# A two-block transformer on one core: 16-blocks of the recurrence's inverses solved four head pairs at a time beside the projections, and 512 moving columns in block 1

## The chip, the cores and the metric

The kernel runs on one core of a Trainium2 chip. The metric is the device time of one execution in microseconds (us). Each kernel is run several times and the median counts. Engines are named as in the profile: PE is TensorE, DVE VectorE, ACT ScalarE, POOL GpSimd, and SP the engine whose queue issues the weight loads.

## What is computed

Two blocks follow one another on a sequence of 256 tokens of width 1024. Block 1 has two layers with three branches each (differential attention, a gated spatial unit, windowed attention), whose inputs are one large projection. Block 2 has two layers between four feed-forward stages; its second layer is an RWKV-7 time mix. This is the part of the reference that the larger edit touches:

```python
xr, xw, xk, xv, xa, xg = [h + xx * mu[i] for i in range(6)]
r = xr @ w_r;  k = xk @ w_k;  v = xv @ w_v
a = jax.nn.sigmoid(a0 + (xa @ a1) @ a2)
g = jax.nn.sigmoid(xg @ g1) @ g2
kk = l2_normalize((k * k_k).reshape(B_, L, H, N))
k = k * (1 + (a - 1) * k_a)
...
def step(S, inp):
    r_t, w_t, k_t, v_t, a_t, b_t = inp
    sa = jnp.einsum('bhvk,bhk->bhv', S, a_t)
    S = S * w_t[:, :, None, :] + sa[..., None] * b_t[:, :, None, :] + v_t[..., None] * k_t[:, :, None, :]
    return S, jnp.einsum('bhvk,bhk->bhv', S, r_t)
```

The recurrence has 16 heads of 64 and 272 steps (16 extra tokens stand ahead of the 256). The kernel computes it in five chunks of 64 steps; within a chunk the dependence of each step on the earlier ones is a triangular system, and its inverse is formed explicitly.

## The kernel before

Activations stay in SBUF, features on partitions: `h` is 128 x 8 x 272. Each weight matmul is three fp32r matmuls, of a high and a low half of either side (`mm3`, L218 to L220; in pinned stretches the same instructions carry L96, and in block 1 `proj_tok` issues them itself). Weights stream in units of 128x1024 f32: SP loads `wraw`, ACT copies the high half `wh` (L210), and DVE, or POOL where the stream says so, subtracts to get the low half `wl` (L212). A unit feeds 24 matmuls. There are four `wraw` buffers and three each of `wh` and `wl`.

A scheduler orders the instructions of each engine, except those pinned to program order. The stages in the profiled execution, in us from the span's start, are: block 1 (9 to 636), a feed-forward (640 to 832), the hybrid layer (832 to 1055), two feed-forwards (1055 to 1467), the RWKV layer's front (1467 to 1602), its eight head pairs (1602 to 1812), its output projection (1812 to 1838), and the last feed-forward with the final norm.

**Block 1.** `proj_tok` forms token-major projections, seven per layer in two layers: each has two PSUM tiles of 128 x 512, and writes half of one (256 columns, two pieces of 128) per matmul.

**The RWKV front.** Projections k, r and v take eight units each, those of the two-step gates (`lora`) a few more. Their inputs are mixes of neighbouring tokens (`mixt` L1523 on DVE; the low half `xl` or `xml` L1526 on DVE and POOL by turns). Behind the decay gate stand a scan (L1565, DVE) and two POOL operations on `D_all` (L1567, L1568). Then kk is normalised and multiplied out (`kt` L1599, `kp` L1600, `kk` L1601 on DVE, `ba_all` L1602 on POOL).

**The head pairs.** A loop runs `stage_b(s-1)`, `stage_c(s-3)`, `stage_a(s)` for eight pairs, so that pairs overlap. `stage_a` makes the decayed operands (L1664 to L1669), the matrix products of a chunk (L1677) with their masked copies (L1681 keeps the 16-blocks in `fk`, L1684, L1687), and sums the 16-blocks into `Uc` (L1690). `stage_b` is `tri_inverse`: the copy L920 and 15 steps of three DVE operations each (L923 to L925) invert the 16-blocks of one pair, 128 partitions x 5 chunks x 16; L927 spreads them into `iY`, and PE and DVE double them to 32 and 64 (L937 to L951). `stage_c` runs the state through the chunks (L1720 to L1737) and normalises (L1743 on); its last instruction is L1763 on POOL.

The steps of the elimination, whose width grows by five elements each:

```python
for j in range(15, 0, -1):
    sh = T(c, pool, [n, ni, 16], F32, f"ish{par}", bufs=2)[:, :, j:]
    nc.vector.stream_shuffle(sh, Yc[:, :, j:], [(p // 16) * 16 + j for p in range(32)])
    nc.vector.tensor_mul(sh, sh, Uc[:, :, j:j + 1].to_broadcast([n, ni, 16 - j]))
    nc.vector.tensor_add(Yc[:, :, j:], Yc[:, :, j:], sh)
```

Of the kernel before, what the change touches and what calls it, by code (L numbers as in the profile page):

```python
# [371 lines left out]
def block1_layer(c, l, xT, head, pos, ws, w_br, w_out, sgu_w, sgu_b, sgu_gb):  # L372
# [14 lines left out]
    def proj_tok(evac):

        pss = [bank(c), bank(c)]
        for p in range(2):  # L390
            for kh in range(2):
                wh, wl = next_unit()
                wh4 = wh.rearrange("p (m k c) -> p m k c", m=2, k=4)
                wl4 = wl.rearrange("p (m k c) -> p m k c", m=2, k=4)
                for i in range(2):
                    o = pss[i][:, 256 * p:256 * p + 256].rearrange("p (m c) -> p m c", m=2)
                    for k4 in range(4):
                        k = 4 * kh + k4
                        a, b = xh[:, k, P * i:P * i + P], xl[:, k, P * i:P * i + P]
                        h, w = wh4[:, :, k4, :], wl4[:, :, k4, :]  # L400
                        pe.matmul(o, a, h, start=k == 0, stop=False)
                        pe.matmul(o, a, w, start=False, stop=False)
                        pe.matmul(o, b, h, start=False, stop=k == 7)
                        if p and kh and k4 == 3:
                            evac(i, pss[i])
                        yield
# [503 lines left out]
def tri_inverse(c, pool, U, Uc, n, ni, levels, nl=None, ybufs=1, tag="sm", par="", pe=None, waits=(0, 0)):  # L910
# [8 lines left out]
    Yc = T(c, pool, [n, ni, 16], F32, f"iYc{par}")  # L919
    nc.vector.tensor_copy(Yc, c.e16[:n].unsqueeze(1).to_broadcast([n, ni, 16]))  # L920
    for j in range(15, 0, -1):
        sh = T(c, pool, [n, ni, 16], F32, f"ish{par}", bufs=2)[:, :, j:]
        nc.vector.stream_shuffle(sh, Yc[:, :, j:], [(p // 16) * 16 + j for p in range(32)])  # L923
        nc.vector.tensor_mul(sh, sh, Uc[:, :, j:j + 1].to_broadcast([n, ni, 16 - j]))  # L924
        nc.vector.tensor_add(Yc[:, :, j:], Yc[:, :, j:], sh)  # L925
# [553 lines left out]
def rwkv(c, h, acc, a):  # L1479
# [20 lines left out]
    with ExitStack() as fst:  # L1500
# [40 lines left out]
        def proj8(q, x, nm):
            for j in range(KT):
                ps = proj(*wrkv.unit(KT * q + j), x)
                nc.scalar.activation(tok(nm, j), ps, AF.Copy)

# [41 lines left out]

        keep = tc.keep_in_program_order
        keep(nc.scalar.preload_act_table_set("natural_log_exp_and_others"))
        for j in range(KT):  # L1590
            ps = bank(c, "sm")
            nc.tensor.matmul(ps[:, :TOK2], c.bo, tok("g", j), start=True, stop=True)
            keep(nc.scalar.activation(tok("g", j), ps[:, :TOK2], AF.Ln, bias=c.eps1))
            keep(nc.scalar.activation(tok("g", j), tok("g", j), AF.Exp, scale=-0.5))
        proj8(2, mix(3), "v")

        for j in range(KT):
            t = T(c, fp, [P, TOK2], F32, "kt1", bufs=2)
            nc.vector.tensor_scalar(t, tok("ba", j), col(c, "k_a", j), c.hc[:, 2, j:j + 1], ALU.mult, ALU.add)  # L1599
            nc.vector.tensor_mul(tok("kp", j), tok("kk", j), t)  # L1600
            nc.vector.scalar_tensor_tensor(tok("kk", j), tok("kk", j), col(c, "k_k", j), tok("g", j), ALU.mult, ALU.mult)  # L1601
            nc.gpsimd.tensor_mul(tok("ba", j), tok("ba", j), tok("kk", j))  # L1602
# [361 lines left out]
```

## Time and profile before

| | |
|---|---|
| median of 3 runs | 2035.62 us (2034.56 to 2041.07) |
| the profiled execution | 2033.22 us, span 2031.5 us, mean granted PE clock 0.964 |
| PE busy | 1929.5 us, 95% of the span, 15003 matmuls |
| DVE busy | 1390.8 us, 68% |
| ACT busy | 973.2 us, 48% |
| POOL busy | 285.1 us, 14% |
| RWKV front and pairs | 1467 to 1812 us of the span |

Busy PE time is modelled for pipelined matmuls, so prices of matmuls are read from the distance between the starts of neighbours. A busy time on DVE or POOL includes what an instruction waited for within itself. The clock is a share of the full 2.4 GHz: 0.5 is 1.2 GHz.

### The profile page before, as it was taken

The page shows a single profiled execution, that of the slowest core. Times are in us where ns is not written, and L with a number is a line of the kernel's source. Part 1 is how long each engine was busy: PE and PEld are TensorE (multiplying, and loading weights), DVE is VectorE, ACT ScalarE, POOL GpSimd, SP SyncE. Part 2 cuts the span into 40 slices and gives each one's busy share as a digit, 9 for nine tenths or more (in the row PEclk, how much of TensorE's full clock was granted, in tenths as well). Part 3 has the DMA queues.
Part 4 walks back from the last instruction along what each step waited for, and adds up shares of the span by engine and source line. Part 5 has one row for each costly group of instructions (what it writes and reads, how often), then busy time and mean ns, then how long its engine had stood idle before and what let it go on. Part 6 is the DMA issues. An engine that isn't in the chain of part 4 may idle for free.

```text
span 2031.5 us, 37801 instructions
## 1 busy us (share of the span) xinstructions
PE 1929.5 (95%) x15003; PEld 1858.0 (91%) x15003; DVE 1390.8 (68%) x2896; ACT 973.2 (48%) x1745; POOL 285.1 (14%) x320
## 2 busy tenths in 40 slices
PE   8999999999999999968999999999989879989998
PEld 7889999889999999966999999999988768979998
DVE  6577576577578665787477665666589699846764
ACT  5455355455355444442354444444366535555443
POOL 1113011113010000143010000000044313110000
PEclk9999899999899999987999999999989789989999
DMA  6445466445455555532235555555534100026663
GB/s 200 137 123 160 142 180 181 142 117 161 141 177 176 177 175 174 164 107 63 63 112 169 175 175 176 171 175 174 171 94 135 42 12 1 32 72 180 186 186 115
DMA packets 79461, 280.02 MB, mean 138 GB/s; under 512 B 9890, under 2 KB 12082, under 8 KB 79156
## 3 DMA queue, kind: packets, MB, share of 16 engines
q1 hardware_dynamic: 77088, 275.57, 45.5%
q8 instruction: 118, 1.93, 0.4%
q10 hardware_dynamic: 2196, 2.03, 0.3%
q14 instruction: 59, 0.48, 0.1%
HBM read 276.50 MB, written 1.07 MB: 137 GB/s over the span
## 4 chain that ended last, share of the span: by engine, by line
PE 64%; DVE 9%; ACT 2%; POOL 2%; issue 1%; DVEq 0%; ACTq 0%; POOLq 0%
PE mm L220 17%; PE mm L218 16%; PE mm L219 16%; PE mm L96 4%; PE iv L96 1%; PE iv L946 1%; DVE wl L212 1%; PE fs L96 1%; PE sm L1677 1%; DVE mixt L1523 1%; DVE iYc L925 1%; DVE ish L924 1%; DVE ish L923 0%; PE sm L264 0%; ACT wh L210 0%
## 5 line engine op out<-in xcount | busy, mean ns | idle before, releaser
L210 ACT ACTIVATE wh<-wraw 128x1024 fp32r<-128x1024 f32 x517 | 546.9, 1059 | 603.6 <-PE mm L219 288.8
L212 DVE TENSOR_TENSOR wl<-wraw,wh 128x1024 fp32r<-128x1024 f32 x474 | 587.1, 1239 | 254.9 <-ACT wh L210 249.6
L218 PE MATMUL mm<-xh,wh 128*128 128x272 f32 (+1 forms) x2112 | 607.4, 288 | 5.9 <-ACT xh L1524 3.0
L220 PE MATMUL mm<-xh,wl 128*128 128x272 f32 (+1 forms) x2112 | 606.2, 287 | 6.6 <-DVE wl L212 2.9
L219 PE MATMUL mm<-xl,wh 128*128 128x272 f32 (+1 forms) x2112 | 606.9, 287 | 0.9 <-POOL xl L1526 0.9
L220 PEld LDWEIGHTS mm<-xh,wl 128*128 128x128 f32 x2112 | 401.5, 190 | 9.0 <-DVE wl L212 5.1
L218 PEld LDWEIGHTS mm<-xh,wh 128*128 128x128 f32 x2112 | 399.7, 189 | 7.9 <-ACT xh L1524 3.5
L219 PEld LDWEIGHTS mm<-xl,wh 128*128 128x128 f32 x2112 | 401.1, 190 | 1.9 <-POOL xl L1526 1.3
L218 PE MATMUL mm<-uh,wh 128*128 128x272 f32 (+1 forms) x704 | 201.7, 286 | 0.0
L219 PE MATMUL mm<-ul,wh 128*128 128x272 f32 (+1 forms) x704 | 201.5, 286 | 0.0
L220 PE MATMUL mm<-uh,wl 128*128 128x272 f32 (+1 forms) x704 | 201.0, 286 | 0.0
L212 POOL TENSOR_TENSOR wl<-wraw,wh 128x1024 fp32r<-128x1024 f32 x43 | 103.0, 2396 | 412.4 <-ACT wh L210 368.8
L96 PE MATMUL mm<-wh,xh 128*128 128x256 f32 x448 | 133.9, 299 | 9.2 <-ACT wh L210 9.2
L220 PEld LDWEIGHTS mm<-uh,wl 128*128 128x128 f32 x704 | 133.2, 189 | 0.0
L218 PEld LDWEIGHTS mm<-uh,wh 128*128 128x128 f32 x704 | 132.3, 188 | 0.0
L219 PEld LDWEIGHTS mm<-ul,wh 128*128 128x128 f32 x704 | 132.3, 188 | 0.0
L96 PE MATMUL mm<-wl,xh 128*128 128x256 f32 x448 | 127.4, 284 | 0.7 <-DVE wl L212 0.7
L96 PE MATMUL mm<-wh,xl 128*128 128x256 f32 x448 | 126.6, 283 | 0.0
L96 PE MATMUL mm<-xh,wh 128*128 128x272 f32 (+1 forms) x360 | 120.0, 333 | 0.0
L96 PE MATMUL mm<-xh,wl 128*128 128x272 f32 (+1 forms) x360 | 107.0, 297 | 0.0
L96 PE MATMUL mm<-xl,wh 128*128 128x272 f32 (+1 forms) x360 | 106.8, 297 | 0.0
L96 PEld LDWEIGHTS mm<-wh,xh 128*128 128x128 f32 x448 | 86.1, 192 | 9.2 <-ACT wh L210 9.2
(597 smaller groups left out, 3576.9 us busy)
## 6 DMA issues: line engine op xcount, KB each, us to landing
wraw<-in_ffn_in SPq DMA_DIRECT2D x176, 512.0 KB, 3.6
wraw<-in_w_in SPq DMA_DIRECT2D x136, 512.0 KB, 3.7
wraw<-in_ffn_out SPq DMA_DIRECT2D x88, 512.0 KB, 3.7
wraw<-in_hyb_in SPq DMA_DIRECT2D x29, 512.0 KB, 3.7
wraw<-in_w_br SPq DMA_DIRECT2D x24, 512.0 KB, 3.8
wraw<-in_rw_rkv SPq DMA_DIRECT2D x24, 512.0 KB, 3.8
wraw<-in_w_out SPq DMA_DIRECT2D x16, 512.0 KB, 4.4
wraw<-in_hyb_out SPq DMA_DIRECT2D x8, 512.0 KB, 3.7
```

What stands on the lines that cost most here:

```text
L96: return lambda *a, **k: self.tc.keep_in_program_order(f(*a, **k))
L210: nc.scalar.activation(wh, r, AF.Copy)
L212: eng.tensor_sub(wl, r, wh.bitcast(F32))
L218: pe.matmul(ps, lh, rh, start=start, stop=False)
L219: pe.matmul(ps, lh, rl, start=False, stop=False)
L220: pe.matmul(ps, ll, rh, start=False, stop=stop)
L924: nc.vector.tensor_mul(sh, sh, Uc[:, :, j:j + 1].to_broadcast([n, ni, 16 - j]))
L925: nc.vector.tensor_add(Yc[:, :, j:], Yc[:, :, j:], sh)
L946: pe.matmul(ps[:n, n * i:n * i + n], lhs[:, i0 + i, :], rhs[:, i0 + i, :], start=True, stop=True)
L1523: nc.vector.scalar_tensor_tensor(t, xx[:, k, :], col(c, "mu", 8 * i + k), hn[:, k, 1:], ALU.mult, ALU.add)
L1677: nc.tensor.matmul(ps[:, P * q:P * q + P], pair_ht(bd[:, c0 + q]), pair_ht(AR[:, c0 + q]), start=True, stop=True)
```

## The change

**Block 1.** `proj_tok` writes 512 contiguous moving columns per matmul, a whole PSUM tile, instead of 256 in two pieces: 48 matmuls per call instead of 96, over the same four units. The host lays the units out accordingly (two k-blocks by four column blocks each).

**The RWKV layer.** The elimination leaves `tri_inverse` and becomes the generator `eliminate`. For the head pairs it runs in the front, for four pairs at once on a tile of 128 x 20 x 16: the first group five steps at a time in the last three turns of the loop over r's units, the second two steps per unit of v. What it needs is made there too: `normed(j)` and `blocks(j)` run per pair in the loop over r, where `blocks` has two exponentials (ACT), three products (DVE), five matmuls of 64 columns, the masked copy out of PSUM and the sum into `Uc` (DVE). `stage_a` loses the masked copy and the sum, but not the decayed operands, which are made a second time. The addend `kt` moves from DVE to ACT. The `wl` subtractions of r's and v's sixteen units move from DVE to POOL. In program order r moves behind the gates' projections. The hybrid layer calls the same `eliminate` in one piece, as before.

```diff
-        for p in range(2):
-            for kh in range(2):
-                wh, wl = next_unit()
...
-                    o = pss[i][:, 256 * p:256 * p + 256].rearrange("p (m c) -> p m c", m=2)
...
+        for kq in range(4):
+            wh, wl = next_unit()
+            for i in range(2):
+                for k2 in range(2):
+                    k = 2 * kq + k2
+                    a, b = xh[:, k, P * i:P * i + P], xl[:, k, P * i:P * i + P]
+                    h, w = wh[:, 512 * k2:512 * k2 + 512], wl[:, 512 * k2:512 * k2 + 512]
+                    pe.matmul(pss[i], a, h, start=k == 0, stop=False)
+                    pe.matmul(pss[i], a, w, start=False, stop=False)
+                    yield
+                    pe.matmul(pss[i], b, h, start=False, stop=k == 7)
...
+def eliminate(c, pool, Uc, Yc, n, ni):
+
+    nc = c.nc
+    nc.vector.tensor_copy(Yc, c.e16[:n].unsqueeze(1).to_broadcast([n, ni, 16]))
+    for j in range(15, 0, -1):
+        sh = T(c, pool, [n, ni, 16], F32, "ish", bufs=2)[:, :, j:]
+        nc.vector.stream_shuffle(sh, Yc[:, :, j:], [(p // 16) * 16 + j for p in range(32)])
+        nc.vector.tensor_mul(sh, sh, Uc[:, :, j:j + 1].to_broadcast([n, ni, 16 - j]))
+        nc.vector.tensor_add(Yc[:, :, j:], Yc[:, :, j:], sh)
+        yield
...
-        lora1, lora2, wrkv = Stream(c, a["rw_lora1"]), Stream(c, a["rw_lora2"]), Stream(c, a["rw_rkv"])
+        lora1, lora2 = Stream(c, a["rw_lora1"]), Stream(c, a["rw_lora2"])
+        wrkv = Stream(c, a["rw_rkv"], lambda u: u >= KT)
...
+        def normed(j):
...
+            nc.scalar.activation(t, tok("ba", j), AF.Identity, scale=col(c, "k_a", j), bias=c.hc[:, 2, j:j + 1])
+            nc.vector.tensor_mul(tok("kp", j), tok("kk", j), t)
...
+        def blocks(j, Uc):
+
+            D = Dall[:, j]
+            E1 = T(c, fp, [P, NCH, 64], F32, "lds", bufs=2)
+            nc.scalar.activation(E1, D[:, :, :64], AF.Exp)
+            E2 = T(c, fp, [P, NCH, 64], F32, "ldc", bufs=2)
+            nc.scalar.activation(E2, D[:, :, 1:], AF.Exp, scale=-1.0)
+            nc.vector.scalar_tensor_tensor(E1, chv("kk", j), -1.0, E1, ALU.mult, ALU.mult)
+            for q in range(2):
+                s = slice(64 * q, 64 * q + 64)
+                nc.vector.tensor_mul(bbd[s, :, q, :], chv("ba", j)[s], E2[s])
+            ps = bank(c, "sm")
+            for q in range(NCH):
+                nc.tensor.matmul(ps[:, 64 * q:64 * q + 64], bbd[:, q].rearrange("p h t -> p (h t)"), E1[:, q],
+                                 start=True, stop=True)
+            U16 = T(c, fp, [P, NCH, 64], F32, "U16")
+            nc.vector.tensor_mul(U16, ps[:, :RT].rearrange("p (c t) -> p c t", t=64),
+                                 c.m16.unsqueeze(1).to_broadcast([P, NCH, 64]))
+            nc.vector.tensor_reduce(Uc, U16.rearrange("p i (b c) -> p i c b", c=16), AX.X, ALU.add)
+
+        Ucs = [T(c, fp, [P, 4 * NCH, 16], F32, f"Uc{i}") for i in range(2)]
+        steps = []
+        for j in range(KT):
+            normed(j)
+            if j >= 1:
+                blocks(j - 1, Ucs[(j - 1) // 4][:, NCH * ((j - 1) % 4):NCH * ((j - 1) % 4) + NCH])
+            if j == 5:
+                steps = eliminate(c, fp, Ucs[0], Ycs[0], P, 4 * NCH)
+            for _ in range(5):
+                next(iter(steps), None)
+            ps = proj(*wrkv.unit(KT + j), xr)
+            nc.scalar.activation(tok("r", j), ps, AF.Copy)
+        blocks(7, Ucs[1][:, 3 * NCH:])
+        steps = eliminate(c, fp, Ucs[1], Ycs[1], P, 4 * NCH)
+        for j in range(KT):
+            for _ in range(2):
+                next(steps, None)
+            ps = proj(*wrkv.unit(2 * KT + j), xv)
+            nc.scalar.activation(tok("v", j), ps, AF.Copy)
```

**Where the order shows it.** The first place is DVE in the front while PE works on v. Before, in this stretch (`kt`, `kp`, `kk` as above, `mixt` and `xml` for the input of the last gate):

```order
L1599 TENSOR_SCALAR kt_3232_18561<-ba_all_17238,cols_80,hcols_16531 128x272
L1601 SCALAR_TENSOR_TENSOR kk_3002_17252<-kk_3002_17252,cols_80,g_all_17241 128x272
L1600 TENSOR_TENSOR kp_3011_17261<-kk_3003_17253,kt_3232_18561 128x272
L1523 SCALAR_TENSOR_TENSOR mixt_18568<-xx_17305,cols_80,hn_17304 128x272
L212 TENSOR_TENSOR wl_18433<-wraw_18430,wh_18432 128x1024
L1601 SCALAR_TENSOR_TENSOR kk_3003_17253<-kk_3003_17253,cols_80,g_all_17241 128x272
L1526 TENSOR_TENSOR xml_18567<-mixt_18568,xmh_18566 128x272
L1523 SCALAR_TENSOR_TENSOR mixt_18572<-xx_17305,cols_80,hn_17304 128x272
```

In the changed kernel, where the lines of `eliminate` are L913 to L915 and the two groups' tiles are the two `Yc`:

```order
L913 STREAM_SHUFFLE ish_17887<-Yc_3013_16608 128x20x15
L913 STREAM_SHUFFLE ish_17940<-Yc_3014_16609 128x20
L914 TENSOR_TENSOR ish_17887<-ish_17887,Uc_3176_17420 128x20x15
L914 TENSOR_TENSOR ish_17940<-ish_17940,Uc_3177_17421 128x20
L915 TENSOR_TENSOR Yc_3013_16608<-Yc_3013_16608,ish_17887 128x20x15
L915 TENSOR_TENSOR Yc_3014_16609<-Yc_3014_16609,ish_17940 128x20
L913 STREAM_SHUFFLE ish_17944<-Yc_3014_16609 128x20x2
L914 TENSOR_TENSOR ish_17944<-ish_17944,Uc_3177_17421 128x20x2
```

The stretch now holds the end of the first group's elimination and, from the second step on, the second group's alone; the low halves `wl` of v are gone from it, and those of the last two gate units come at the second group's steps 11 and 13.

The second place is POOL at the same time. Before (`ba_all` is the last product of the normalisation, the MEMSET clears tiles for the pairs):

```order
L1602 TENSOR_TENSOR ba_all_17238<-ba_all_17238,kk_3002_17252 128x272
L1602 TENSOR_TENSOR ba_all_17238<-ba_all_17238,kk_3003_17253 128x272
L1526 TENSOR_TENSOR xml_18567<-mixt_18572,xmh_18566 128x272
L1526 TENSOR_TENSOR xml_18567<-mixt_18580,xmh_18566 128x272
L1526 TENSOR_TENSOR xml_18567<-mixt_18588,xmh_18566 128x272
L1526 TENSOR_TENSOR xml_18567<-mixt_18596,xmh_18566 128x272
L1644 MEMSET wraw_18757 128x640
```

In the changed kernel, from r's third unit on (`ba_all` is L1614 there):

```order
L212 TENSOR_TENSOR wl_17548<-wraw_17545,wh_17547 128x1024
L1614 TENSOR_TENSOR ba_all_16566<-ba_all_16566,kk_2998_16576 128x272
L212 TENSOR_TENSOR wl_17605<-wraw_17602,wh_17604 128x1024
L212 TENSOR_TENSOR wl_17662<-wraw_17659,wh_17661 128x1024
L212 TENSOR_TENSOR wl_17740<-wraw_17737,wh_17739 128x1024
L1614 TENSOR_TENSOR ba_all_16566<-ba_all_16566,kk_2999_16577 128x272
L212 TENSOR_TENSOR wl_17817<-wraw_17814,wh_17816 128x1024
L1614 TENSOR_TENSOR ba_all_16566<-ba_all_16566,kk_3000_16578 128x272
```

POOL's row now carries the sixteen 128x1024 subtractions of r and v among the eight `ba_all` products, each of which the blocks of a pair wait for.

## Rows read from the trace of the kernel before

**Rows 1.** Windows: stretch, its length, busy us (instructions) of PE, PEld, DVE, ACT, POOL, PE clock, DMA share, GB/s

```profile
1526.90:1591.40 64.50, 60.29 (x437) 58.69 (x438) 58.60 (x89) 42.36 (x82) 31.14 (x29) 0.95 0.42 131
1602.00:1676.00 74.00, 56.21 (x320) 48.96 (x321) 63.79 (x309) 26.07 (x67) 14.78 (x20) 0.73 0.02 8
1676.00:1755.00 79.00, 74.46 (x594) 68.89 (x593) 73.30 (x328) 44.21 (x126) 21.93 (x28) 1.00 0.03 8
1755.00:1812.00 57.00, 47.74 (x363) 43.39 (x362) 22.85 (x69) 28.31 (x79) 12.07 (x16) 0.97 0.12 38
```

**Rows 2.** Timeline of PE in block 1: start us, us, engine, line, operation

```profile
11.09 0.41 PE L96 MATMUL mm<-wh,xh 128*128 128x256 f32 x1
...
16.43 0.41 PE L96 MATMUL mm<-wl,xh 128*128 128x256 f32 x1
...
30.73 0.28 PE L96 MATMUL mm<-wl,xh 128*128 128x256 f32 x1
...
37.44 0.28 PE L96 MATMUL mm<-wl,xh 128*128 128x256 f32 x1
```

**Rows 3.** Windows: one stretch of a feed-forward, columns as in the first group

```profile
700.00:800.00 100.00, 100.00 (x800) 100.00 (x799) 63.45 (x90) 48.11 (x65) 0.00 (x0) 1.00 0.59 175
```

**Rows 4.** Timeline of POOL, 112 to 116 us

```profile
112.88 2.37 POOL L212 TENSOR_TENSOR wl<-wraw,wh 128x1024 fp32r<-128x1024 f32 x1 [16.85 <-ACT wh L210]
```

**Rows 5.** Timeline of DVE, the same stretch

```profile
113.09 2.44 DVE L484 SCALAR_TENSOR_TENSOR gate<-gt,ga 128x256 f32<-128x256 f32 x1
```

**Rows 6.** Source line L484: count, min/median/max ns, first and last start

```profile
L484 DVE SCALAR_TENSOR_TENSOR gate<-gt,ga x12: 410/418/2483, 113.1 to 267.2; 128x256 f32<-128x256 f32 x12
```

**Rows 7.** Timeline of DVE in the hybrid layer, its elimination

```profile
932.61 0.20 DVE L923 STREAM_SHUFFLE ish<-iYc 96x36 f32<-96x36 f32 x1
...
933.31 0.20 DVE L923 STREAM_SHUFFLE ish<-iYc 96x48 f32<-96x48 f32 x1
...
946.57 1.66 DVE L924 TENSOR_TENSOR ish<-ish,iUc 96x120 f32<-96x120 f32 x1
...
948.59 0.31 DVE L923 STREAM_SHUFFLE ish<-iYc 96x132 f32<-96x132 f32 x1
...
949.26 0.29 DVE L925 TENSOR_TENSOR iYc<-iYc,ish 96x132 f32<-96x132 f32 x1
```

**Rows 8.** Timeline of DVE in the front (neighbours of one kind merged, xcount)

```profile
1542.34 2.35 DVE L212 TENSOR_TENSOR wl<-wraw,wh 128x1024 fp32r<-128x1024 f32 x2
...
1559.56 0.78 DVE L1600 TENSOR_TENSOR kp<-kk,kt 128x272 f32<-128x272 f32 x2
...
1602.28 0.49 DVE L1664 SCALAR_TENSOR_TENSOR wh<-kk,E 128x320 f32<-128x320 f32 x1 [6.32 <-ACT E L1654]
```

**Rows 9.** Lines of DVE in the pairs, xcount | busy us, mean ns | idle before

```profile
L925 DVE TENSOR_TENSOR iYc<-iYc,ish 128x50 f32<-128x50 f32 (+14 forms) x120 | 28.7, 252 | 0.9
L924 DVE TENSOR_TENSOR ish<-ish,iUc 128x50 f32<-128x50 f32 (+14 forms) x120 | 27.9, 244 | 0.6
L923 DVE STREAM_SHUFFLE ish<-iYc 128x70 f32<-128x70 f32 (+14 forms) x118 | 22.4, 203 | 0.0
...
L1665 DVE TENSOR_TENSOR bbd<-ba_all,E 64x320 f32<-64x320 f32 x16 | 9.4, 586 | 0.8 <-PE sm L1696 0.5
...
L1690 DVE TENSOR_REDUCE iUc<-fk 128x80 f32<-128x320 f32 x8 | 5.5, 688 | 0.0
L1681 DVE TENSOR_TENSOR fk<-sm,m 128x256 f32<-128x256 f32 (+1 forms) x16 | 5.0, 315 | 2.3 <-PE sm L1677 2.3
```

**Rows 10.** Source line L1743 in the pairs

```profile
L1743 PE MATMUL ch<-ysb,cm x16: 392/394/497, 1676.3 to 1803.1; 128*128 128x272 f32 x16
```

**Rows 11.** Timeline of POOL, the end of pair 4

```profile
1762.90 0.76 POOL L1763 TENSOR_TENSOR kp<-yc,kk 128x272 fp32r<-128x272 f32 x1 [0.54 <-ACT kk L1762]
```

**Rows 12.** Source line L1763 in the pairs

```profile
L1763 POOL TENSOR_TENSOR kp<-yc,kk x8: 757/762/937, 1685.9 to 1811.4; 128x272 fp32r<-128x272 f32 x8
```

More of the change, by code (lines that the diff above doesn't have):

```diff
@@ L389, in proj_tok @@
         pss = [bank(c), bank(c)]
-        for p in range(2):
-            for kh in range(2):
-                wh, wl = next_unit()
-                wh4 = wh.rearrange("p (m k c) -> p m k c", m=2, k=4)
-                wl4 = wl.rearrange("p (m k c) -> p m k c", m=2, k=4)
-                for i in range(2):
-                    o = pss[i][:, 256 * p:256 * p + 256].rearrange("p (m c) -> p m c", m=2)
[L397 to L406, printed above, removed]
+        for kq in range(4):
[9 more added lines that the diff above has]
+                    pe.matmul(pss[i], b, h, start=False, stop=k == 7)
+                    if k == 7:
+                        evac(i, pss[i])
+                    yield
     def rope_T(res, scale):
@@ L918, in tri_inverse @@
     g = 4
[L919 to L925, printed above, removed]
     Y = T(c, pool, [n, ni, n], F32, "iY", bufs=ybufs)
@@ L1350, in chain @@
         nonlocal og
-        Y = yield from tri_inverse(c, ap, U, compact16(c, ap, U, CH, 12), CH, 12, (16, 32, 64), tag="iv", pe=pe,
-                                   waits=(80, 2))
+        Uc = compact16(c, ap, U, CH, 12)
+        Yc = T(c, ap, [CH, 12, 16], F32, "iYc")
+        for _ in eliminate(c, ap, Uc, Yc, CH, 12):
+            pass
+        Y = yield from tri_inverse(c, ap, U, Yc, CH, 12, (16, 32, 64), tag="iv", pe=pe, waits=(80, 2))
         nW = T(c, ap, [P, 4, 2, CH], F32, "nW")
@@ L1493, in rwkv @@
     nc.gpsimd.memset(Dall[:, :, 4, 17:], -1.0)
+    Ycs = [T(c, ap, [P, 4 * NCH, 16], F32, f"Yc{i}") for i in range(2)]
     flat = lambda n, j, m: S1[n][j][:, :m] if n in S1 else S3[n][:, TOK2 * j:TOK2 * j + m]
@@ L1539, in proj @@
             return proj_n([(wh, wl)], x)[0]
[L1541 to L1544, printed above, removed]
         e05 = -0.5 * math.exp(-0.5)
@@ L1568, in lora_wa @@
                 nc.gpsimd.tensor_scalar(Dall[:, j, :, 0:1], y[:, :, 31:32], -1.0, None, ALU.mult)
+        keep = tc.keep_in_program_order
         xk = mix(2, True)
@@ L1586, in rwkv @@
         lora_wa(1)
[L1588 to L1602, printed above, removed]
         xg = mix(5)
@@ L1611, in rwkv @@
         keep(nc.scalar.preload_act_table_set("natural_log_exp_and_others"))
+        xr, xv = mix(0), mix(3)
+        bbd = T(c, fp, [P, NCH, 2, 64], F32, "bbd0")
+        nc.gpsimd.memset(bbd, 0.0)
+        def normed(j):
+            ps = bank(c, "sm")
+            nc.tensor.matmul(ps[:, :TOK2], c.bo, tok("g", j), start=True, stop=True)
+            g = tok("g", j)
+            keep(nc.scalar.activation(g, ps[:, :TOK2], AF.Ln, bias=c.eps1))
+            keep(nc.scalar.activation(g, g, AF.Exp, scale=-0.5))
+            t = T(c, fp, [P, TOK2], F32, "kt1", bufs=2)
+            nc.scalar.activation(t, tok("ba", j), AF.Identity, scale=col(c, "k_a", j), bias=c.hc[:, 2, j:j + 1])
+            nc.vector.tensor_mul(tok("kp", j), tok("kk", j), t)
+            nc.vector.scalar_tensor_tensor(tok("kk", j), tok("kk", j), col(c, "k_k", j), g, ALU.mult, ALU.mult)
+            nc.gpsimd.tensor_mul(tok("ba", j), tok("ba", j), tok("kk", j))
@@ L1826, in b1_host @@
         if nm[1] in "qkv":
-            for p in range(2):
-                for kh in range(2):
-                    order += [(4 * kh + k4, base[nm] + 2 * p + m) for m in range(2) for k4 in range(4)]
+            order += [(k, base[nm] + m) for k in range(8) for m in range(4)]
         else:
```

15 lines of the change are left out of this document (5 added, 10 removed).

## Prediction

> **What bounds the kernel now.** The timelines come first, because PE is busy nearly everywhere and the price of a matmul must be known. In block 1, neighbouring matmuls of 256 columns start 0.2136 us apart at the beginning ((16.43 − 11.09)/25, the first and last of 26 rows) and 0.1177 us apart once warm ((37.44 − 30.73)/57, of 58 rows) [rows 2]. The first is 256 columns at 1.2 GHz, 213 ns, and nothing beside them. At 2.4 GHz the columns alone are 106.7 ns, so each warm matmul costs 11 ns that don't go with its columns. A feed-forward confirms it: 800 matmuls of 272 columns in 100 us are 125.0 ns each, where the columns alone are 113.3 [rows 3]. Block 1 and the feed-forwards run as such streams; PE bounds them.
>
> The windows of the RWKV layer look different [rows 1]. From 1526.9 to 1591.4 us, 64.5 us in which r, v and the a gate are computed, PE is busy for 60.3 and DVE for 58.6: two engines near their limit. The start of the pairs, 74 us from 1602, has DVE at 63.8, PE at 56.2 and a clock of 0.73. In the middle (79 us) both are full, PE 74.5 and DVE 73.3 at clock 1.00. At the end (57 us) DVE has only 22.9.
>
> The DVE lines of the pairs say what fills it: three operations of the elimination, 120 times each, 28.7 + 27.9 + 22.4 = 79 us of busy time, on 5 to 75 elements at 0.2 to 0.25 us apiece: mostly fixed cost [rows 9]. The change attacks that fixed cost.
>
> **How DVE and POOL meet.** A low half on POOL takes 2.37 us from 112.88 [rows 4]. A DVE product with two SBUF inputs that starts at 113.09, inside it, takes 2.44 us and ends with it [rows 5]; the same line's twelve have a median of 0.418 and a largest of 2.483 [rows 6]. The elimination's product at 946.57 shows the same, 1.66 where its neighbours take 0.3 [rows 7]. So work with two SBUF inputs on DVE and work on POOL are done by turns, and the elimination's products and sums are of this kind. The Trainium skill (GPSIMD Engine Reference, Key points) says so: GpSimd shares its SBUF interfaces with VectorE, and VectorE instructions with two SBUF inputs contend. The trace agrees, 2.44 against 0.42 us.
>
> **Part 1, block 1.** 14 calls of 96 matmuls become 14 of 48: 672 fewer, the columns unchanged. With 11 ns each, 672 × 11 = 7.4 us; a 512-column matmul isn't in the trace. Bounds: nothing, if the extra goes with columns after all, and 8. The two widths at hand (256 and 272) differ by 7.3 ns where 16 columns are 6.7, so the extra is close to a constant, and I take **−7**. Units, ACT's and DVE's work and the count of yields stay, so nothing else moves there. The Trainium skill (TensorE: Matmul & The Clock Gate, Back-to-back issue gap) puts the isolated gap at the columns plus 2.5 ns. By that the term would be 672 × 2.5 = 1.7 us, an estimate from that page; the rows show 11 ns, and the measurement decides.
>
> **Part 2, the front.** Up to 1526.9 us little differs. Then, per engine, up to the end of the second group's elimination:
>
> - DVE loses sixteen low halves at 2.35/2 = 1.18 us [rows 8], 18.9, and the eight `kt`, some 2.
> - DVE gains `blocks`: eight products of 320 elements like the one at 1602.28, 0.49 [rows 8], 3.9; sixteen half products, 5.9 (9.4 busy in the pairs, with waits inside [rows 9]; at 0.78/2 us for 272 elements [rows 8] they are 6 to 7); masked copies, 3.6 to 5.0, and sums, 5.5 [rows 9]. Together about 19. The two gate operations that move ahead of this point give 2.
> - DVE gains two eliminations on 20 to 300 elements. The hybrid's shows steps of 0.70 us at 36 elements (932.61 to 933.31) and 1.00 at 132 (948.59 to the end of its sum, 949.26 + 0.29, and 0.04 to the next) [rows 7]. A line through both is 0.59 + 0.0031 per element; over 15 steps with a mean of 160 elements, 16.3 per group, 32.6 for both. The 79 us of the pairs shrink to that.
> - POOL gains sixteen low halves at 2.4 [rows 4], 38.4.
>
> DVE: −21 + 19 + 2 + 32.6 = +32.6. If POOL ran freely beside it, the stretch would be DVE's 58.6 + 32.6 = 91 us. If every added microsecond of both took its turn, 64.5 + 32.6 + 38.4 = 135.5. Not all do: the 30 shuffles have one input and are not held (0.31 us at 132 elements [rows 7], about 9 in all), neither are the copies and sums out of PSUM, and DVE idled for 5.9 before. I take 15 off: 120.5, so the eliminations end near 1647. The last gate units' subtractions stand at the end of that row, and behind them PE has 48 matmuls for g, 6 us; the pairs can start near 1653, where they started at 1602 [rows 8]. **+51**, bounds +21 (free) and +66 (by turns throughout). Work on PE doesn't set this: r, v, the a gate and the last gate are the same matmuls as before, and the 40 of `blocks` are small. But PE will wait. On its row the five matmuls of `blocks` wait for DVE's half products, and r's next unit is queued behind them; on POOL's row the low halves of r stand between `ba_all` products that wait for DVE's `kk`, and what is queued behind those, down to v's units, PE waits for in turn. Two edits cost nothing of their own. ACT gets sixteen exponentials and eight `kt`, each about one pass over 320 or 272 elements, and was busy for 42.4 of 64.5 us [rows 1]: it hides them in a stretch twice as long, and would cost some 10 us if that cover were gone. On SP's queue the loads of r's units now follow those of the gates; at a DMA share of 0.42 [rows 1] and four buffers they are there before DVE and POOL get to them.
>
> **Part 3, the pairs.** They lose 79 + 5.5 + 5.0 = 90 us of busy DVE time. What it is worth:
>
> - The fill. The first norm starts at 1676.3 [rows 10] and pair 0 ends at 1685.9 [rows 12], 84 us after the start. Pair 0's elimination, 15 dependent steps of 0.6 to 0.7 us with others' work between, is gone from it, and so is pair 1's, which shares DVE with it. I take −20; bounds −10 (its own chain) and −30 (DVE's share, 63.8 of 74, down by two pairs' 20 and more).
> - The slots. From pair 0's end to pair 4's (1762.9 [rows 11]) four pairs take 77.0, 19.2 each. PE's share there is 74.46/79, so 18.1 of each is PE's own. DVE no longer presses, PE does: −2, at most −4.
> - The drain. Pairs 5 to 7 take 48.5, up to 1811.4 [rows 12]. The last elimination sits in the first of them: −4, bounds 0 and −7.
>
> Together **−26**, bounds −12 and −41.
>
> **The sum.** +51 − 26 − 7 = +18. The profiled execution took 2033.22 us, 2.4 below the median of the runs; 2035.6 + 18 gives 2053.6. I say **2053**: the elimination becomes cheaper by 46 us of DVE time, in a place that had no free time and that at the same time is given 38 us of POOL's work, where 19 of DVE's would do.
>
> **The rivals.**
>
> - *Faster: POOL works beside DVE.* The low halves start when ACT and the buffers allow, not always against a product, and while POOL waits DVE goes on; what speaks for it is that the shuffles and PSUM operations need no turn. At +21 for the front, 2035.6 + 21 − 26 − 7 = 2024, and with the larger gain in the pairs (−36) 2014. Against it stand the held rows. It decides if the front grows by less than 33. Chance 0.24.
> - *About even.* The overlap of turns is twice what I took off (30 of the added 71), the front grows by 36, and the pairs give 30: 2035.6 + 36 − 30 − 7 = 2035. Chance 0.15.
> - *Slower still: turns throughout, and the fill keeps its length.* PE waits in v, falls to a clock of 0.5, and starts the pairs cold; the start of the pairs was at 0.73 already [rows 1], so only 12 come back: 2035.6 + 66 − 12 − 7 = 2083. Against it: the shuffles need no turn. Chance 0.06.
> - *Block 1 gives nothing* (the 11 ns go with columns): 7 us later in each case, 2060 for the likeliest. It changes no sign but the even one's.
>
> **Numbers.** My forecast with its bounds, 2042 to 2070, has 0.55, of which 2042 is a front of 41 with the pairs as forecast, and 2070 the full 66. With the case above it, slower has 0.61, same 0.15, faster 0.24. Within 0.3%, 6 us, a measurement of this kernel tells no change. The range runs from 2016, which leaves out the lower part of the faster case, to 2070.
>
> **What would show it.** Right: in the profile after, POOL's `wl` rows in r and v, DVE products and sums of `eliminate` of 1 to 2.5 us among ones of 0.3 to 0.45, PE waiting for `wl` of POOL or for `blocks`, the first pair product about 50 us later than now while block 1 ends 7 earlier, and the pairs' length near 184 instead of 210. Block 1's matmuls would start 0.224 us apart. Wrong: a front that ends before 1635 less block 1's gain (turns don't cost), pairs shorter than 170 (DVE had been the limit in the drain, too), or 0.235 in block 1 (a pair of old matmuls).

## The result and the profile after

The changed kernel takes 2065.19 us, the median of 4 runs (2061.98 to 2070.15), against 2035.16 for the kernel before: 1.0143 times, with a 95% interval of 1.0115 to 1.0171. It is 30 us slower. The profiled execution is the slowest of the four, 2070.15 us with a span of 2068.4.

The windows of the RWKV layer in the changed kernel, columns as in [rows 1]; the first four are the front from the end of the scan on, the last three the head pairs:

```profile
1526.00:1560.00 34.00, 23.16 (x119) 20.68 (x119) 30.58 (x55) 21.90 (x50) 19.69 (x19) 0.72 0.20 62
1560.00:1600.00 40.00, 27.52 (x172) 26.52 (x173) 31.65 (x48) 18.95 (x38) 22.87 (x14) 0.79 0.26 80
1600.00:1640.00 40.00, 31.82 (x215) 31.23 (x214) 35.27 (x76) 11.83 (x19) 19.98 (x12) 0.83 0.24 78
1640.00:1668.00 28.00, 21.85 (x94) 17.14 (x92) 16.67 (x54) 5.78 (x15) 2.83 (x5) 0.63 0.06 19
1668.00:1715.00 47.00, 38.64 (x296) 35.52 (x295) 33.99 (x73) 22.75 (x59) 13.47 (x16) 0.93 0.05 12
1715.00:1802.00 87.00, 85.72 (x688) 80.02 (x686) 47.61 (x105) 52.65 (x149) 27.11 (x36) 1.00 0.05 13
1802.00:1849.00 47.00, 38.14 (x288) 34.67 (x288) 11.82 (x24) 22.07 (x61) 9.56 (x13) 0.96 0.11 35
```

Where [rows 1] had PE busy for 60.3 of 64.5 us in the front, it is now busy for 23 of 34, 28 of 40, 32 of 40 and 22 of 28, at clocks down to 0.63. The middle of the pairs is the reverse: PE busy for 85.7 of 87 us with DVE at 47.6, where DVE stood at 73.3 of 79 before.

The first and last starts of four lines of the changed kernel, columns as in [rows 6]: the front's first operation, the first exponential of the pairs, the pairs' norm matmuls, the last operation of a pair:

```profile
L1528 DVE SCALAR_TENSOR_TENSOR hn<-h,cols,R x8: 487/496/877, 1469.8 to 1480.4; 128x272 f32<-128x272 f32 x8
...
L1697 ACT ACTIVATE E<-D_all x8: 458/474/478, 1667.5 to 1755.4; 128x325 f32<-128x325 f32 x8
...
L1780 PE MATMUL ch<-ysb,cm x16: 392/393/497, 1714.3 to 1840.1; 128*128 128x272 f32 x16
...
L1800 POOL TENSOR_TENSOR kp<-yc,kk x8: 755/762/773, 1724.9 to 1848.4; 128x272 fp32r<-128x272 f32 x8
```

The front, from the first to the second of these, is 1667.5 − 1469.8 = 197.7 us; in the kernel before it was 130.7 (1471.1 to 1601.8). The pairs, up to the start of the last L1800, are 180.9 where they were 209.6 [rows 12]. So the front grew by 67.0, the pairs shrank by 28.7, and the stages ahead gave 1.3 in this execution: 37, the difference of the two profiled executions.

What stands against the front's length shows in three views. Waits in it (who waits for whom: us in total, times, longest):

```profile
PE sm L1629 <- DVE bbd L1626: 21.2, 6, 6.1
...
POOL ba_all L1614 <- DVE kk L1613: 15.9, 7, 5.6
...
DVE U L1632 <- PE sm L1629: 8.5, 6, 2.2
```

DVE's groups (columns as in [rows 9]), then POOL's, in the same stretch:

```profile
L1626 DVE TENSOR_TENSOR bbd<-ba_all,ldc 64x320 f32<-64x320 f32 x16 | 18.3, 1146 | 2.5 <-POOL ba_all L1614 2.4
...
L1623 DVE SCALAR_TENSOR_TENSOR lds<-kk,lds 128x320 f32<-128x320 f32 x8 | 6.7, 838 | 0.1
...
L914 DVE TENSOR_TENSOR ish<-ish,Uc 128x280 f32<-128x280 f32 x2 | 3.1, 1542 | 0.1
...
L913 DVE STREAM_SHUFFLE ish<-Yc 128x280 f32<-128x280 f32 x2 | 1.0, 512 | 0.0
...
L915 DVE TENSOR_TENSOR Yc<-Yc,ish 128x280 f32<-128x280 f32 x2 | 0.9, 450 | 0.1
```

```profile
L212 POOL TENSOR_TENSOR wl<-wraw,wh 128x1024 fp32r<-128x1024 f32 x16 | 40.5, 2536 | 21.2 <-ACT wh L210 21.2
```

The half products of `blocks` take 1.146 us on average; the same ones in the pairs took 0.586 [rows 9]. The elimination's product at 280 elements takes 1.542, while its sum, of the same width, takes 0.450, and the shuffle 0.512. The timeline of DVE and then of POOL says why:

```profile
1626.71 0.43 DVE L914 TENSOR_TENSOR ish<-ish,Uc 128x260 f32<-128x260 f32 x1
...
1628.19 2.63 DVE L914 TENSOR_TENSOR ish<-ish,Uc 128x280 f32<-128x280 f32 x1
```

```profile
1628.12 2.40 POOL L212 TENSOR_TENSOR wl<-wraw,wh 128x1024 fp32r<-128x1024 f32 x1 [6.87 <-ACT wh L210]
```

The product at 260 elements takes 0.43 us. The one at 280 starts 0.07 after a low half on POOL, and ends when that has ended: 2.63. Fifteen of the sixteen low halves hold a DVE operation in this way, by 1.1 to 2.2 us each; added up over the timeline, about 29 us of DVE's row.

Last, block 1's matmuls in the timeline of PE, the first and last of 41 in one row:

```profile
29.84 0.40 PE L96 MATMUL mm<-wh,xh 128*128 128x512 f32 x1
...
39.13 0.39 PE L96 MATMUL mm<-wl,xh 128*128 128x512 f32 x1
```

That is 0.2322 us apart (9.29/40). Two of the old ones are 2 × 0.1177 [rows 2].

### The profile page after: what moved, and what is told of

It is laid out like the page before. It is cut to its first block, busy times and chain, and to the rows that moved or that the text cites. A ratio compares the mean times of both kernels' runs of the same rounds, so it can differ in the third digit from the quotient of the medians.

```text
span 2068.4 us, 36302 instructions
## 1 busy us (share of the span) xinstructions
PE 1945.6 (94%) x14411; PEld 1838.1 (89%) x14411; DVE 1375.4 (66%) x2522; ACT 981.6 (47%) x1768; POOL 324.0 (16%) x337
## 4 chain that ended last, share of the span: by engine, by line
PE 82%; DVE 9%; POOL 3%; ACT 3%; issue 2%; DMA 0%; DVEq 0%; POOLq 0%; ACTq 0%
PE mm L218 18%; PE mm L220 18%; PE mm L219 18%; PE mm L96 13%; PE sm L96 2%; PE iv L96 1%; DVE wl L212 1%; PE iv L948 1%; PE po L96 1%; PE sm L1719 1%; PE fs L96 1%; DVE mixt L1531 1%; POOL wl L212 1%; DVE bbd L1626 1%; DVE ish L914 1%
## 5 line engine op out<-in xcount | busy, mean ns | idle before, releaser
L212 DVE TENSOR_TENSOR wl<-wraw,wh 128x1024 fp32r<-128x1024 f32 x458 | 565.3, 1234 | 250.2 <-ACT wh L210 244.9
L218 PE MATMUL mm<-xh,wh 128*128 128x272 f32 (+1 forms) x2056 | 594.7, 290 | 5.9 <-ACT xh L1532 3.0
L220 PE MATMUL mm<-xh,wl 128*128 128x272 f32 (+1 forms) x2056 | 592.7, 288 | 7.2 <-POOL wl L212 5.7
L219 PE MATMUL mm<-xl,wh 128*128 128x272 f32 (+1 forms) x2056 | 593.5, 289 | 2.7 <-POOL xl L1534 1.7
L220 PEld LDWEIGHTS mm<-xh,wl 128*128 128x128 f32 x2056 | 393.7, 192 | 9.1 <-POOL wl L212 6.5
L212 POOL TENSOR_TENSOR wl<-wraw,wh 128x1024 fp32r<-128x1024 f32 x59 | 147.8, 2505 | 426.0 <-ACT wh L210 392.7
L96 PE MATMUL mm<-xh,wh 128*128 128x272 f32 (+1 forms) x360 | 120.4, 334 | 0.0
L96 PE MATMUL mm<-xh,wl 128*128 128x272 f32 (+1 forms) x360 | 107.2, 298 | 0.0
L96 PE MATMUL mm<-xl,wh 128*128 128x272 f32 (+1 forms) x360 | 107.1, 298 | 0.0
L96 PE MATMUL mm<-wh,xh 128*128 128x512 f32 x224 | 95.3, 426 | 9.0 <-ACT wh L210 9.0
L269 POOL TENSOR_TENSOR rtok<-ms,mhalf 128x2 f32<-128x2 f32 (+1 forms) x10 | 8.1, 805 | 553.5 <-DVE ms L266 534.9
L219 PE MATMUL mm<-yl,wh 128*128 128x256 f32 x320 | 91.3, 286 | 0.5 <-DVE yl L228 0.5
L220 PE MATMUL mm<-yh,wl 128*128 128x256 f32 x320 | 90.7, 284 | 0.0
```

Of the source, the lines that this page charges most:

```text
L96: return lambda *a, **k: self.tc.keep_in_program_order(f(*a, **k))
L212: eng.tensor_sub(wl, r, wh.bitcast(F32))
L218: pe.matmul(ps, lh, rh, start=start, stop=False)
L219: pe.matmul(ps, lh, rl, start=False, stop=False)
L220: pe.matmul(ps, ll, rh, start=False, stop=stop)
L269: nc.gpsimd.tensor_tensor(r[:, :nt], ms[:, :nt], c.mhalf[:, :nt], ALU.pow)
```

## The experiments

Three theories stood against each other first. **Turns**: POOL's sixteen low halves cost their length on DVE's path. **Beside**: POOL works freely next to DVE, and its work costs nothing. **Chain**: the blocks' matmuls wait for POOL, DVE and PE by turns with r queued behind them, and POOL's work is only cover. Two more came up on the way: **PE's cover**, that r's place between the gates had kept PE busy, and **DVE's row**, that its total work sets the front. Totals move with what comes ahead of the front, which began anywhere between 1460 and 1473 us in the profiled executions, so the lengths of front and pairs are given too, measured as above, each in one profiled execution. Each ratio is to runs of the kernel before that were taken together with that kernel's; their medians lie between 2032 and 2035, and it is formed over all runs, so it can differ a little from the quotient of two medians.

| kernel | median us | ratio to before, interval | front | pairs |
|---|---|---|---|---|
| before | 2035.16 | | 130.7 | 209.6 |
| changed | 2065.19 | 1.0143, 1.0115 to 1.0171 | 197.7 | 180.9 |
| 1 block 1 alone | 2029.92 | 0.9981, 0.9966 to 0.9995 | 131.4 | 207.4 |
| 2 low halves on DVE | 2032.61 | 0.9986, 0.9968 to 1.0005 | 158.3 | 185.8 |
| 3 before, low halves on POOL | 2052.44 | 1.0074, 1.0049 to 1.0099 | 150.2 | 207.5 |
| 4 second group left out | 2057.14 | 1.0104, 1.0078 to 1.0129 | 186.2 | 182.7 |
| 5 r ahead of blocks | 2069.59 | 1.0194, 1.0139 to 1.0249 | 195.0 | 182.7 |
| 6 POOL for v alone | 2047.45 | 1.0090, 1.0061 to 1.0119 | 179.3 | 181.6 |
| 7 second group later | 2033.79 | 1.0002, 0.9977 to 1.0027 | 158.2 | 185.4 |
| 8 and mixes on DVE | 2034.13 | 1.0004, 0.9979 to 1.0030 | 159.8 | 185.4 |
| 9 before, r late | 2045.37 | 1.0054, 1.0034 to 1.0074 | 142.1 | 208.4 |
| 10 half of r back | 2026.20 | 0.9957, 0.9940 to 0.9974 | 156.8 | 182.8 |
| 11 last gate earlier | 2031.34 | 0.9993, 0.9972 to 1.0015 | 158.1 | 184.7 |

**1. Block 1 alone.** The kernel before with the new `proj_tok` and the host's order for it, nothing else.

> Only block 1's edit, on the kernel before. Constant theory (11 ns beside the columns of every warm matmul, so 672 fewer matmuls save them): 7 us faster, 2028. Width theory (the extra grows with the columns; in the changed kernel 512-column matmuls start 0.2322 us apart, a pair of the old ones 0.2354): 2 us faster, 2033, inside what a measurement can tell.

It gave 4 us, 1 to 7 by the interval. The 7.4 of the constant theory lies just outside, the 2 of the width theory inside. Over all profiled executions the front begins 6 us earlier with the edit than without (1465 as the mean of ten, 1471 of three), but they scatter by 10. Block 1 itself scatters less: the first matmul behind it, the first of 272 columns, starts between 628.5 and 629.5 us in the three without the edit and between 623.5 and 626.9 in the ten with it, 3.8 us earlier on the mean. So the gain of about 4 us is real and arises in block 1.

**2. Low halves on DVE.** The changed kernel, and:

```diff
-        wrkv = Stream(c, a["rw_rkv"], lambda u: u >= KT)
+        wrkv = Stream(c, a["rw_rkv"])
```

> The changed kernel, with the low halves of r and v back on DVE. Turns theory (POOL's 38 us of low halves cost their length on DVE's path, DVE does them in 19): the front shortens by 15 to 25 us, 2040 to 2050. Chain theory (the front is long because the matmuls of each pair's blocks wait for a chain POOL, DVE, PE, DVE, with the next unit of r queued behind them; POOL's work is cover): 0 to 5 us faster, 2060 to 2065. Beside theory (POOL's work costs nothing and relieves DVE): 10 to 19 us slower, 2075 to 2085.

The whole loss is gone, more than any of the theories said: the front is 39.4 us shorter. Windows of its front after the scan:

```profile
1520.00:1550.00 30.00, 20.74 (x103) 19.53 (x104) 29.16 (x56) 23.08 (x52) 14.18 (x16) 0.67 0.20 57
1550.00:1580.00 30.00, 29.45 (x214) 28.61 (x214) 28.88 (x57) 19.34 (x40) 6.34 (x7) 0.93 0.40 119
1580.00:1600.00 20.00, 19.38 (x157) 19.19 (x157) 18.82 (x51) 7.20 (x11) 1.68 (x3) 1.00 0.51 155
1600.00:1621.00 21.00, 19.96 (x123) 17.04 (x121) 19.52 (x68) 8.21 (x17) 3.33 (x6) 0.88 0.08 30
```

DVE is busy for 96 of 101 us and PE for 90; in the changed kernel it was 114 and 104 of 142. So 18 of the 41 us are DVE's row, and 23 are time in which DVE idled. Where the two fronts part shows when they are cut at the first of the 48 matmuls for g, the last work of the front; from the end of the last scan to there and from there to the pairs, the changed kernel first:

```profile
1528.70:1645.00 116.30, 87.50 (x544) 83.42 (x545) 99.38 (x194) 52.72 (x107) 60.32 (x41) 0.80 0.23 73
1645.00:1667.50 22.50, 16.35 (x52) 11.84 (x51) 12.23 (x34) 3.49 (x10) 2.35 (x4) 0.56 0.08 23
...
1520.90:1609.20 88.30, 78.78 (x544) 76.53 (x545) 84.86 (x185) 53.17 (x107) 22.27 (x25) 0.87 0.32 96
1609.20:1620.30 11.10, 10.76 (x50) 7.84 (x48) 9.95 (x44) 3.48 (x10) 2.35 (x4) 0.80 0.13 48
```

28.0 us lie ahead of g's matmuls and 11.4 in them. In the changed kernel PE waits there for two low halves of the gate's units, 4.2 and 1.9 us, which stand on DVE's row between steps of the second group (in run 2 the last of them stands right behind its first step); after the first of these waits the clock is at 0.50 up to the pairs, and DVE has nothing left to do for the last 9.5 us.

PE's waits from the scan to the first pair:

```profile
PE mm L219 <- DVE z1l L228: 5.5, 1, 5.5
PE mm L220 <- DVE wl L212: 5.0, 2, 2.8
...
PE sm L1629 <- DVE bbd L1626: 1.2, 2, 0.6
```

The 21.2 us in front of the blocks' matmuls are 1.2 now: they went with POOL's low halves.

**3. The low halves on POOL, in the kernel before.**

```diff
+        wrkv = Stream(c, a["rw_rkv"], lambda u: u >= KT)
```

> The kernel before, with only the low halves of r and v moved to POOL. Turns theory: 64.5 us of front grow by 38 - 19 = 19, less what finds idle time, 8 to 19 us slower, 2043 to 2054. Beside theory: the front gets shorter or stays, 2030 to 2036. Chain theory says nothing of it: no blocks here; 0 to 8 us slower.

First operation of the front and first exponential of the pairs:

```profile
L1521 DVE SCALAR_TENSOR_TENSOR hn<-h,cols,R x8: 486/496/877, 1472.9 to 1483.5; 128x272 f32<-128x272 f32 x8
...
L1655 ACT ACTIVATE E<-D_all x8: 458/476/477, 1623.0 to 1735.6; 128x325 f32<-128x325 f32 x8
```

1623.0 − 1472.9 = 150.2 with the unrounded starts, 19.5 more than before, where the sum has 38 − 19. The beside theory is out, by this edit alone, and so is the chain as the whole cause, for there are no blocks here. The agreement with 19 is closer than the mechanism is. From the last scan to the pairs, in the kernel before and in this one:

```profile
1529.70:1601.80 72.10, 68.32 (x484) 64.71 (x483) 58.49 (x101) 47.78 (x94) 30.85 (x30) 0.95 0.39 124
...
1533.70:1623.00 89.30, 73.54 (x487) 69.05 (x486) 67.81 (x85) 48.37 (x94) 56.35 (x44) 0.89 0.34 101
```

Of the 17.2 us by which this stretch grew, DVE's row took 9.3, and in 7.9 DVE idled. PE waits 8.9 us there for POOL's low halves.

**4. The second group left out.** The changed kernel, with one step of that elimination.

```diff
-            for _ in range(2):
+            if j == 0:
                 next(steps, None)
```

> The changed kernel without 14 of the 15 steps of the second group's elimination; the inverses of pairs 4 to 7 are therefore not those of the reference. If DVE's row sets the end of the front (turns theory), its 15 us and what they wait for come off, 15 to 22 us faster, 2043 to 2050. If the chain of the blocks sets it, v's projection alone remains behind it and PE needs 24 us for that: 5 to 10 us faster.

The time falls by 8 us, inside the second range, and the front by 11.5. The same two stretches as in run 2 show where:

```profile
1526.10:1642.30 116.20, 88.39 (x543) 84.31 (x544) 94.37 (x169) 52.83 (x107) 60.18 (x41) 0.80 0.23 73
1642.30:1654.00 11.70, 11.70 (x52) 8.71 (x51) 1.31 (x3) 3.47 (x9) 2.35 (x4) 0.75 0.15 46
```

Up to g's matmuls nothing changed (116.2 against 116.3), though DVE had 5 us less to do there. From there on the stretch is 11.7 instead of 22.5: the second group's steps held up the low halves of the last gate, and that is what the front felt of them. So DVE's row as a whole doesn't set the length of the changed front.

**5. r ahead of the blocks.** In the loop over r, `proj` and its copy stand ahead of `normed` and `blocks`.

> The changed kernel (low halves on POOL), with each turn of the loop over r issuing r's 24 matmuls ahead of the pair's normalisation and blocks. Chain theory: PE no longer waits 21 us in front of the blocks' matmuls, 12 to 20 us faster, 2045 to 2053. Turns theory: DVE and POOL need the same time, the wait moves to another place, 0 to 6 us faster, 2059 to 2065.

PE's order changed by one unit: between the first and the second set of the blocks' matmuls stand 46 of r's where 17 stood, and the later sets follow one another with about a unit between them, as before. Its wait did not change:

```profile
PE sm L1629 <- DVE bbd L1626: 21.0, 6, 5.8
```

The front is 195.0 against 197.7. The median, 2070, lies above both ranges, with an interval that overlaps that of the changed kernel. The chain theory had this relieve the wait, and it does not. But units and blocks still alternate on PE, so this run does not exclude that the chain adds to what the turns cost.

**6. POOL for v alone.** `lambda u: u >= 2 * KT`.

> The changed kernel with r's low halves on DVE and v's still on POOL. Moving all sixteen gave 30 us. Turns theory: each of them costs alike, so half comes back, 2045 to 2052. Chain theory: r's are those that stand between the products of the chain, so nearly all comes back, 2035 to 2041.

18.4 us of front come back with r's eight low halves (197.7 to 179.3), and 21.0 were left for v's (to 158.3). By the total each half costs alike, as the turns theory said, but not in the same place:

```profile
1521.90:1620.50 98.60, 82.03 (x543) 79.53 (x544) 94.26 (x194) 53.32 (x107) 41.72 (x32) 0.85 0.27 86
1620.50:1642.30 21.80, 16.41 (x52) 11.89 (x51) 14.02 (x41) 3.52 (x10) 2.35 (x4) 0.57 0.07 25
```

Against run 2's stretches, r's eight cost 17.7 us ahead of g's matmuls (116.3 to 98.6), 2.2 each, and 0.7 in them. v's cost 10.3 ahead of them (98.6 to 88.3), 1.3 each, close to run 3's 1.2, and 10.7 in them (21.8 to 11.1). That the halves come out alike is partly chance.

**7. The second group later.** All low halves on DVE, and:

```diff
-        steps = eliminate(c, fp, Ucs[1], Ycs[1], P, 4 * NCH)
...
+    steps = eliminate(c, pp, Uc1, Ycs[1], P, 4 * NCH, chunk_t(w7[:, 512:832], 16))
     for s in range(KT + 3):
+        if 1 <= s <= 4:
+            for _ in range(4):
+                next(steps, None)
```

> All low halves on DVE, and the second group's elimination issued with the first head pairs (it is needed from pair 4 on), in one buffer. DVE theory (DVE's row is the front's limit, 97 of 101 us busy with the low halves on DVE): the front, 158 us there, loses what of the 16 us leaves it, some 8 to 14, the pairs take them in where DVE is half idle: 2019 to 2026. If PE is the limit there (busy for 89 of the same 101): 0 to 4 us, 2029 to 2033.

The front stays at 158.2. The scheduler still fills DVE's row with the group's cheaper steps ahead of the pairs; but no microsecond of the front hung on the others. Its windows from the scan on:

```profile
1519.00:1549.00 30.00, 21.50 (x106) 20.29 (x107) 29.20 (x56) 23.38 (x52) 14.20 (x15) 0.67 0.21 67
1549.00:1579.00 30.00, 29.46 (x217) 28.60 (x216) 28.88 (x60) 18.87 (x40) 5.56 (x7) 0.94 0.34 109
1579.00:1611.00 32.00, 31.39 (x244) 30.31 (x243) 30.16 (x90) 12.28 (x21) 5.00 (x8) 1.00 0.35 116
```

After the first stretch PE is busy for 60.9 of 62 us: it is the limit there. In the first it is busy for 21.5 of 30, at 0.67.

**8. And the mixes' low halves on DVE.** `eng = nc.vector` in `mix`.

> As the run before, and the low halves of the mixes, half of them on POOL, all on DVE: 24 operations of 0.39 us on DVE in place of 24 of 0.87 on POOL. Turns theory: 5 to 11 us faster than that run. Beside theory: up to 9 us slower, DVE gets 24 x 0.39 more.

No change: the turns theory misses, and the DVE work that was added doesn't show in the time (its front is 1.6 us longer). It is of a piece with the run before: DVE's row doesn't set this front.

**9. r late, in the kernel before.** The projections of the a gate and the last gate and their mixes are issued ahead of r's, as in the changed kernel; with r, the norms of kk and v's projection also come behind the last gate's, and one load of an ACT table falls away. The work on PE stays.

> The kernel before, with only the order of the front changed: both gates' projections ahead of r, as in the changed kernel. Cover theory (PE starves between the gates when r's 24 us don't stand there; with the low halves on DVE PE was busy for 21.5 of 30 us at a clock of 0.67 in that place): the front, 130.7 us, grows by 10 to 16, 2043 to 2049. If the order is free (DVE's row sets the time, and does the same work): within 4 us, 2029 to 2037.

```profile
L1520 DVE SCALAR_TENSOR_TENSOR hn<-h,cols,R x8: 486/494/878, 1469.5 to 1480.1; 128x272 f32<-128x272 f32 x8
...
L1654 ACT ACTIVATE E<-D_all x8: 458/475/478, 1611.5 to 1724.9; 128x325 f32<-128x325 f32 x8
```

142.1 us of front, 11.4 more. Between the gates, where r's projection stood, PE starves; behind them it is full:

```profile
1525.00:1555.00 30.00, 23.41 (x127) 21.24 (x128) 27.74 (x53) 20.54 (x46) 12.83 (x12) 0.79 0.28 88
1555.00:1587.00 32.00, 31.39 (x247) 30.90 (x246) 26.95 (x36) 17.51 (x32) 13.71 (x13) 1.00 0.53 166
```

This order is worth 11 us.

**10. Half of r back.** Run 7, with four of r's units between the gates, and the loop with blocks beside r's other four and v's first four.

```diff
         lora_wa(0)
+        xr = mix(0)
+        for j in range(4):
+            ps = proj(*wrkv.unit(KT + j), xr)
+            nc.scalar.activation(tok("r", j), ps, AF.Copy)
         ps = proj(*lora1.unit(1), mix(4))
```

> The run with all low halves on DVE and the second group later, with four of r's eight units back between the two gates; the loop with blocks then runs beside the other four of r and the first four of v. Cover theory: the front (158 us) loses 8 to 14, 2019 to 2026, faster than the kernel before. DVE theory (DVE busy for 88 of 92 us there, the same work in another order): 0 to 5 us, 2028 to 2034.

It is the fastest, 0.43% below the kernel before and about 38 us below the changed one. But the front gave 1.4, not 8 to 14:

```profile
1520.00:1550.00 30.00, 26.28 (x161) 25.26 (x161) 27.71 (x50) 20.82 (x45) 13.30 (x13) 0.79 0.36 122
1550.00:1580.00 30.00, 26.73 (x190) 24.66 (x188) 27.39 (x52) 22.43 (x47) 10.04 (x10) 0.94 0.27 88
1580.00:1612.00 32.00, 29.63 (x204) 27.44 (x202) 29.74 (x103) 11.04 (x22) 5.93 (x8) 0.93 0.26 83
```

PE is busier in the first window (26.3 of 30, clock 0.79) and less busy after it, 26.7 of 30 and 29.6 of 32. Cover won in one place is lost in the next, and 2.6 come from the pairs. The rest of its lead over run 7 lies ahead of the front or in the scatter of the runs.

**11. The last gate earlier.** Run 10, with the 48 matmuls of g ahead of v's last four units.

> The run with half of r put back, with the last gate's 48 matmuls ahead of v's last four units. They ran at half clock there, 11 us where 48 warm ones need 6, right ahead of the head pairs. If their slow end is what the pairs wait for: front 5 us shorter, 2019 to 2023. If the low clock comes with these matmuls wherever they stand, or DVE's row sets the time: within 2 us of that run, 2024 to 2028.

The front is 158.1: nothing won, and the median, 2031, lies above both ranges. The 48 matmuls ran between v's units, from 1588.7 to 1614.3 us, and the clock was low there too: 0.61 from 1600 to 1615 us, with PE busy throughout. The price of 6 us for them warm was too small as well: in the kernel before they took 8.6 (1592.8 to 1601.4) at 0.95.

## Why the prediction was right, and where it was off

It said slower by 18 us, within 2016 to 2070; it was 30. The reason that it gave for the sign holds: POOL's low halves hold DVE's products, and with them on DVE the loss is gone (2); put into the kernel before, they slow that too (3). That the size came near is in part luck: in the front, terms that were too small stood against one that was too large.

- **Part 1, block 1, −7.** Measured −4, 1 to 7. The step that failed is "the extra is close to a constant": at 512 columns the extra is 0.2322 − 0.2133 = 18.9 ns, not 11. By these starts 672 fewer matmuls give 672 × 3.2 = 2 us. The forecast's own signs had 0.224 for right and 0.235 for wrong, and 0.2322 is nearer the second. Block 1 ends 3.8 us earlier on the mean of the executions (run 1); where the rest beyond these 2 us arises is not settled. The Trainium skill (TensorE: Matmul & The Clock Gate, Back-to-back issue gap) made 1.7 us of it with its constant of 2.5 ns, an estimate. The rows show 3.2 for each matmul saved, and the page was nearer than my 11, though one 512-column matmul has 18.9 beside its columns.
- **Part 2, the front, +51 with bounds 21 and 66.** Measured +67, just above the upper bound. Four terms were off. *The low halves* stood at 38 − 19 = 19. Run 3 shows a growth of 19.5 in the front without blocks; in the changed kernel it was 39.4 (run 2), 2.5 us per low half, of which 11.4 lie in g's matmuls. *r's place* stood at nothing: "Work on PE doesn't set this" was wrong, for the new order costs 11.4 in the kernel before (run 9), with the same work on PE. *Blocks and eliminations* stood at 19 + 32.6 = 51.6, with 15 taken off for overlap. What is left for them is 67.0 − 39.4 − 11.4 = 16, if the three prices add up, which no run shows; PE's eighty rows for the blocks and DVE's work are not told apart in it. *The last gate* stood at 6 us on PE; its stretch took 9.0 in the kernel before and 22.5 in the changed one, where its low halves waited on DVE and the clock fell; this lies within the prices of the other terms.
- **DVE's row as the front's limit**, on which this sum was built, is not borne out. In the changed kernel 5 us less on it ahead of g's matmuls changed nothing there (run 4). With the low halves on DVE the front did not follow DVE's row either (7, 8), though it was busy for 96 of 101 us.
- **Part 3, the pairs, −26 with bounds 12 and 41.** Measured −28.7 in the profiled execution, −22 to −28 in the other runs of that form against 207.4 to 209.6. The fill, to pair 0's end, went from 84.1 to 57.4: −26.7, not −20. The four slots from there took 77.0 (1724.9 to 1801.9), as before: 0, not −2. The drain took 46.5 instead of 48.5: −2, not −4. PE was busy for 85.7 of 87 us in the slots, as forecast, and they were no shorter for it: it had been the limit there already.
- **The rivals.** The faster one asked for POOL to work beside DVE; the timelines show the opposite. Of the one that was slower still, with a chance of 0.06, the front came true (+66 forecast, +67 measured), but not the pairs (−12 against −28.7). The elimination did get cheaper; without POOL's part (run 2) the change stands level with the kernel before, and so the freed DVE time was worth what r's order and the blocks cost. The lower end of the likeliest case, 2042, is a slip: a front of 41 gives 2035.6 + 41 − 26 − 7 = 2043.6.

## What to carry to other kernels

Before work is moved to GpSimd to relieve VectorE, see whether the two take turns: a two-input operation on VectorE that ends with GpSimd's, at five to six times its length, is the sign. The move then costs at least about the difference of the two prices, here 1.2 us each (run 3), and more where other engines wait for what is held, here 2.5 (run 2). A projection that stands between two dependent ones is cover for them; if it moves, count what PE does in its place, even though no work is added. A price that is read at two nearly equal widths (256 and 272) does not tell constant from proportional.

## What was not expected

A low half on POOL cost 1.2 us in the front of the kernel before (19.5/16), the difference of the two engines' prices, and 2.5 in the changed front (39.4/16). Fifteen of them hold a DVE operation, which makes 29 us. DVE also idles for 28 of 142 us there, against 5 of 101 with the low halves on DVE: 8.5 in front of the copies out of the blocks' matmuls (0.8 in run 2), 9.5 at the end, while PE runs g's matmuls at 0.50, and the rest in smaller pieces. The 512-column matmul carries 18.9 ns beside its columns where the 256-column one carries 11: most of that extra goes with the columns, and it is absent at 1.2 GHz, where 256 columns took 213.6 ns [rows 2].
